# Mixing stage of a two-block transformer kernel: the chunked recurrence recast as one state map per chunk and eight-chunk sweeps

## The chip, the core and the metric

The kernel runs on one core of one Trainium2 chip. The metric is the device time of one execution in microseconds: 1955.51 us is the median of three runs of the kernel before (1954.65 to 1956.76). The profiled execution took 1951.49 us.

## What is computed

The input is 512 tokens of width 1024 in fp32. Two transformer blocks follow each other. Only one part of the second block is touched, the RWKV-7 recurrence: eight heads of 64, whose state is a 64 by 64 matrix that is updated at each of the 512 tokens.

```python
def step(state, inp):
    r_t, w_t, k_t, v_t, a_t, b_t = inp
    sa = jnp.einsum('bhvk,bhk->bhv', state, a_t)
    state = (state * w_t[:, :, None, :] + sa[..., None] * b_t[:, :, None, :]
             + v_t[..., None] * k_t[:, :, None, :])
    return state, jnp.einsum('bhvk,bhk->bhv', state, r_t)
```

Beside the recurrence, the same stage computes the input projections of the block, a second attention (stick-breaking, eight heads) and the output projection.

## The kernel before, in words

The kernel works with features on partitions and tokens on the free axis. Large products are "dense" matmuls: weights are split into a high and a low part (ScalarE makes `whi`, line 243, VectorE makes `wlo`, line 249), and each 128 by 128 block of weights meets 512 tokens in three passes that add up in a bank of PSUM called `mm`. PSUM has eight banks: two for `mm`, and in this stage three called `c` and three called `pt`.

**The recurrence in chunks.** The eight heads are taken two at a time, f = 0 to 3: one head on partitions 0 to 63 and one on 64 to 127. The 512 tokens are eight chunks of 64. `rw_solve` (line 1825) prepares one f. After the norms and the decays it turns three tiles into token order (`tok`, line 1868), forms two 64 by 128 matrices per chunk and head (`mat`, line 1901; masked by VectorE at line 1908) and inverts a unit triangular 64 by 64 matrix per chunk and head by doubling: five levels (line 1947), each with a first product (line 1951), a masked copy out of PSUM into `z` by VectorE (line 1955), a second set of products (lines 1961 to 1966), and additions into the running inverse `tmt` by VectorE (lines 1968 to 1974). `rw_scan` (line 1977) then walks through the eight chunks one after another, with three steps that wait for each other in each chunk: the sum of two products goes through ScalarE into `xc` (line 1994), the product with the inverse goes through ScalarE into `uc` (line 2004), and from that come the new state `st` (VectorE, line 2016) and the chunk's output (VectorE, line 2023).

**Corners of the array.** All these products are 64 by 64 in fp32, so each uses one quarter of the 128 by 128 array: rows by the partitions it reads, columns by the partitions it writes. `pair` (line 401) issues two of them, one per head, each from its half to the same half. `four` (line 409) adds two for another chunk whose result goes to the opposite half (`other`, line 418), so that four different corners are used. In the trace each fp32 matmul of this kind stands as two instructions.

**The order of the work.** The instruction order of TensorE is written out by a planner, `weave` (line 425), when the program is built. Its streams are generators: a step issues small products and the copies behind them, then yields the time at which the next step may run, by estimates (`after`, line 468, with the constants of `COST`). While a stream waits, the planner puts dense matmuls in, at least `MINF` = 4 at a time, out of a fixed supply per period (line 1792). `WORK` (line 23) says how much small work it expects in each of five periods, and sets how the dense supply is spread over them. Period f runs the solve of f beside the scan of f - 1; period 4 runs the last scan beside the stick-breaking attention (lines 1813, 1814). TensorE executes strictly in that order, so a small product that isn't ready holds back everything after it.

Of the kernel before, what the change touches and what calls it, by code (L numbers as in the profile page):

```python
# [22 lines left out]
WORK = (28e3, 40e3, 41e3, 40e3, 85e3)  # L23
# [78 lines left out]
def consts2():  # L102
# [16 lines left out]
    for b in (2, 4, 8, 16, 32):  # L119
        lv.append(((q // b % 2 == 1) & (g // b == q // b - 1)))  # L120
# [173 lines left out]
class K:  # L294
# [114 lines left out]
    def four(self, *g):  # L409

        t = self.clock
        for o, l, r in g:
            for hh in (0, 1):
                p = slice(64 * hh, 64 * hh + 64)
                self.mm(o(p), l(p), r(p), start=True, stop=True)
        self.clock = t + 55 + (self.clock - t) / 4

    def other(self, p):
        return slice(64 - p.start, 128 - p.start)

    def turn(self, o, x):

        self.pair(o, x, lambda p: self.ident[p, p], True, True)
# [1401 lines left out]
    def rw_solve(self, f, u, ag):  # L1825
# [42 lines left out]
        def tok(n, src):  # L1868
            ps = self.bank("c")
            for c in range(8):  # L1870
                cs = slice(64 * c, 64 * c + 64)
                self.turn(lambda p: ps[p, cs], lambda p: src[p, cs])
            d = t2(f"tok{n}")
            S.activation(d, ps, AF.Copy)
            self.after("S", 512)
            return d

        yield lambda: (f, 0) in u
# [6 lines left out]
        vt = tok(2, v)  # L1885
# [8 lines left out]
        kt = tok(1, kb)  # L1894
# [6 lines left out]
        def mat(n, src):  # L1901
            for half in (0, 1):
                ps = self.bank("c")
                for c4 in range(4):
                    c = 4 * half + c4
                    self.pair(lambda p: ps[p, 128 * c4:128 * c4 + 128], lambda p: src[p, 64 * c:64 * c + 64],
                              lambda p: ar[p, c].rearrange("p i t -> p (i t)"), True, True)
                V.tensor_tensor(mats[n][:, 4 * half:4 * half + 4], ps.rearrange("p (c n) -> p c n", c=4),
                                C["mar"].unsqueeze(1).to_broadcast([128, 4, 128]), op=OP.mult)
                x = self.after("V", 512)  # L1910
                yield self.clock if half == 0 else x
# [11 lines left out]
        bc = lambda x: x.unsqueeze(1).to_broadcast([128, 4, 64])  # L1923
        sw = self.other
        tt = [self.rp.tile([128, 2, 4, 64], F32, name=f"tmt{q}", tag=f"tmt{q}", bufs=2) for q in (0, 1)]
        zz = lambda q: t2(f"z{q}", 256, 1).rearrange("p (c t) -> p c t", t=64)
        e = zz(1)
        for q, d in ((0, tt[0][:, 1]), (1, e)):
            V.tensor_tensor(d, ab[:, 4 * q:4 * q + 4, 0:64], bc(C["m1t"]), op=OP.mult)
            V.tensor_tensor(d, d, bc(C["eye"]), op=OP.add)  # L1930
            x = self.after("V", 512)
        self.rws = dict(ar=ar, ab=ab, ak=ak, bt=bt, kt=kt, vt=vt, tt=tt, dec=dec, bon=bon)
        eight = lambda: self.bank("c").rearrange("p (i c t) -> p i c t", i=2, t=64)
        da, db = tt
        yield x
        pa, pb = eight(), eight()
        for c in range(4):
            self.turn(lambda p: pa[p, 0, c], lambda p: da[p, 1, c])
        for c in range(4):
            self.four((lambda p: pa[p, 1, c], lambda p: e[p, c], lambda p: self.ident[p, p]),  # L1940
                      (lambda p: pb[sw(p), 0, c], lambda p: self.ident[p, p], lambda p: e[p, c]))
        S.activation(da[:, 0], pa[:, 0], AF.Copy)
        S.activation(db[:, 0], pa[:, 1], AF.Copy)
        w = self.after("S", 512)
        S.activation(db[:, 1], pb[:, 0], AF.Copy)
        self.after("S", 256)
        for l in range(5):
            yield w
            pa, pb = eight(), eight()
            for c in range(4):  # L1950
                self.four((lambda p: pa[p, 0, c], lambda p: ab[p, c, 0:64], lambda p: da[p, 0, c]),
                          (lambda p: pb[sw(p), 0, c], lambda p: ab[p, 4 + c, 0:64], lambda p: db[p, 0, c]))
            za, zb = zz(0), zz(1)
            for z, ps in ((za, pa), (zb, pb)):
                V.tensor_tensor(z, ps[:, 0], bc(C["lev"][:, 64 * l:64 * l + 64]), op=OP.mult)
                w = self.after("V", 256)
            yield w
            pa, pb, pc = eight(), eight() if l < 4 else None, eight()
            if l < 4:
                for c in range(4):  # L1960
                    self.four((lambda p: pa[p, 0, c], lambda p: da[p, 1, c], lambda p: za[p, c]),
                              (lambda p: pb[sw(p), 0, c], lambda p: db[p, 1, c], lambda p: zb[p, c]))
            for c in range(4):
                self.pair(lambda p: pa[p, 1, c], lambda p: za[p, c], lambda p: da[p, 1, c], True, True)
            for c in range(4):
                self.pair(lambda p: pc[p, 0, c], lambda p: zb[p, c], lambda p: db[p, 1, c], True, True)
            if l < 4:
                V.tensor_tensor(da, pa, da, op=OP.add)
                V.tensor_tensor(db[:, 0], pb[:, 0], db[:, 0], op=OP.add)
                self.after("V", 512)  # L1970
            else:
                V.tensor_tensor(da[:, 1], pa[:, 1], da[:, 1], op=OP.add)
            w = self.after("V", 256)
            V.tensor_tensor(db[:, 1], pc[:, 0], db[:, 1], op=OP.add)
            self.after("V", 256)

    def rw_scan(self, f, u, o, g2, sg, w):

        nc, V, S, P, C = self.nc, self.nc.vector, self.nc.scalar, self.nc.gpsimd, self.C2
        ar, ab, ak, bt, kt, vt, tt, dec, bon = (w[k] for k in ("ar", "ab", "ak", "bt", "kt", "vt", "tt", "dec", "bon"))  # L1980
        t2 = self.rt
        st = std = None
        y = o
        for c in range(8):
            cs = slice(64 * c, 64 * c + 64)
            tc = tt[c // 4][:, 1, c % 4]
            at = self.other if c > 3 else lambda p: p
            b = self.bank("pt")[:, 0:64]
            self.pair(lambda p: b[at(p)], lambda p: ak[p, c, 0:64], lambda p: vt[p, cs], True, st is None)
            if st is not None:  # L1990
                yield w
                self.pair(lambda p: b[at(p)], lambda p: ar[p, c, 0], lambda p: st[p], False, True)
            x = t2("xc", 64)
            S.activation(x, b, AF.Copy)
            w = self.after("S", 64)
            if st is not None and c < 7:
                std = t2("std", 64)
                V.tensor_scalar(std, st, dec[:, c:c + 1], None, op0=OP.mult)
                self.after("V", 64)
# [90 lines left out]
```

## Time and profile before

| what | value |
|---|---|
| median of three runs | 1955.51 us |
| profiled execution, its own time | 1951.49 us |
| its span, first to last instruction | 1949.7 us |
| TensorE busy | 1864.8 us, 96% |
| VectorE busy | 1094.1 us, 56% |
| ScalarE busy | 797.5 us, 41% |
| GpSimd busy | 149.9 us, 8% |
| granted TensorE clock, mean | 0.979 |

The profile is of one execution. Busy times are of each engine alone. A matmul's row lasts from its start to its modelled end; the matmuls of one stream overlap, so what one costs is read from start to start. The mixing stage with the recurrence lies at 1165 to 1573 us of the span.

### The profile page before, as it was taken

Reading aid. Unit: us, or ns where it says so; the run is one execution under the profiler, and the core shown is the slowest. Engines: PE = TensorE matmul, PEld = TensorE weight load, DVE = VectorE, ACT = ScalarE, POOL = GpSimd, SP = SyncE. Lnnn points to the kernel's source line nnn. Section 1 sums busy time; section 2 is a strip of 40 time slices with the busy share of each in tenths; the row PEclk is TensorE's granted clock in tenths of the full one; section 3 lists DMA queues with packets and bytes.
Section 4 is the critical chain, followed back from the end, with each engine's and each line's share of the span. In section 5 each row is a group of like instructions: output and inputs, shape, how many; then the busy total and the mean of one; then the engine's idle time right before and its main releaser. Section 6 shows DMA issues by size and latency. Waiting matters only on the chain.

```text
span 1949.7 us, 27795 instructions
## 1 busy us (share of the span) xinstructions
PE 1864.8 (96%) x11552; PEld 1456.1 (75%) x11556; DVE 1094.1 (56%) x1843; ACT 797.5 (41%) x1385; POOL 149.9 (8%) x117
## 2 busy tenths in 40 slices
PE   5989999979999998999999999999999999999999
PEld 2766666758888886788888877776766778888887
DVE  7588875583434345543444556676667774444343
ACT  3666767343323233322322354343445753223231
POOL 4341110050000002000000000000001300000000
PEclk8999999889999998999999999999999999999999
DMA  7124214312223221222232231110100022222222
GB/s 300 57 87 140 78 65 152 113 61 92 103 90 105 89 106 65 87 93 101 88 107 87 89 124 55 45 45 24 40 18 33 22 87 96 99 92 103 92 98 92
DMA packets 27486, 171.56 MB, mean 88 GB/s; under 512 B 3168, under 2 KB 3680, under 8 KB 9184
## 3 DMA queue, kind: packets, MB, share of 16 engines
q1 hardware_dynamic: 23472, 163.44, 24.2%
q10 hardware_dynamic: 3888, 6.34, 1.0%
q8 instruction: 91, 1.49, 0.3%
q14 instruction: 35, 0.29, 0.0%
HBM read 167.67 MB, written 2.10 MB: 87 GB/s over the span
## 4 chain that ended last, share of the span: by engine, by line
PE 77%; DVE 3%; ACT 2%; POOL 1%; issue 1%; DMA 1%; ACTq 0%; POOLq 0%
PE ps_mm L339 43%; PE ps_s L339 23%; PE ps_c L339 5%; PE ps_pt L339 4%; PE ps_o L339 1%; ACT whi L243 1%; DVE wlo L249 1%; POOL xr L1332 0%; PE ps_pt L902 0%; POOL x L1381 0%; DMA mask<-in_mask 0%; DMA x<-in_x 0%; PE ps_mm L758 0%; DVE hl L1396 0%; DVE rs_v L510 0%
## 5 line engine op out<-in xcount | busy, mean ns | idle before, releaser
L243 ACT ACTIVATE whi<-w 128x1024 fp32r<-128x1024 f32 (+4 forms) x277 | 274.7, 994 | 740.7 <-PE ps_mm L339 440.8
L339 PE MATMUL ps_mm<-hh,whi 128*128 128x512 f32 x1304 | 519.9, 400 | 20.9 <-ACT whi L243 9.5
L339 PE MATMUL ps_mm<-hh,wlo 128*128 128x512 f32 x1304 | 518.1, 398 | 6.2 <-DVE wlo L249 6.2
L339 PE MATMUL ps_mm<-hl,whi 128*128 128x512 f32 x1304 | 519.2, 398 | 3.4 <-DVE hl L1339 2.0
L249 DVE TENSOR_TENSOR wlo<-w,whi 128x1024 fp32r<-128x1024 f32 (+7 forms) x316 | 322.3, 1025 | 149.3 <-ACT whi L243 148.8
L339 PEld LDWEIGHTS ps_mm<-hh,whi 128*128 128x128 f32 x1304 | 247.6, 190 | 82.3 <-ACT whi L243 12.8
L339 PEld LDWEIGHTS ps_mm<-hh,wlo 128*128 128x128 f32 x1304 | 247.4, 190 | 65.0 <-DVE wlo L249 10.1
L339 PEld LDWEIGHTS ps_mm<-hl,whi 128*128 128x128 f32 x1304 | 247.4, 190 | 60.3 <-DVE hl L1339 3.5
L339 PE MATMUL ps_s<-vl,whi 128*128 128x512 f32 x352 | 137.2, 390 | 0.0
L339 PE MATMUL ps_s<-vh,wlo 128*128 128x512 f32 x352 | 137.0, 389 | 0.0
L339 PE MATMUL ps_s<-vh,whi 128*128 128x512 f32 x352 | 136.6, 389 | 0.0
L1449 DVE SCALAR_TENSOR_TENSOR x<-ps_s,x 128x512 f32<-128x512 f32 x48 | 33.2, 692 | 129.2 <-PE ps_s L339 129.2
L1437 DVE TENSOR_TENSOR su<-ps_mm,rr 128x512 f32<-128x512 f32 x42 | 29.0, 691 | 133.1 <-PE ps_mm L339 133.1
L339 PE MATMUL ps_s<-uh,whi 128*128 128x512 f32 x256 | 99.6, 389 | 0.0
L339 PE MATMUL ps_s<-ul,whi 128*128 128x512 f32 x256 | 99.6, 389 | 0.0
L339 PE MATMUL ps_s<-uh,wlo 128*128 128x512 f32 x256 | 99.6, 389 | 0.0
L1436 DVE TENSOR_TENSOR sg<-ps_mm,rr 128x512 f32<-128x512 f32 x42 | 29.1, 692 | 97.3 <-PE ps_mm L339 93.2
L339 PEld LDWEIGHTS ps_s<-vl,whi 128*128 128x128 f32 x352 | 66.1, 188 | 14.3 <-DVE vl L783 0.7
L339 PEld LDWEIGHTS ps_s<-vh,wlo 128*128 128x128 f32 x352 | 66.1, 188 | 13.7
L339 PEld LDWEIGHTS ps_s<-vh,whi 128*128 128x128 f32 x352 | 66.1, 188 | 13.7
L876 ACT ACTIVATE P<-ps_s,st 128x512 f32<-128x512 f32 (+2 forms) x96 | 50.1, 528 | 15.7 <-DVE st L874 13.8
L1373 DVE TENSOR_TENSOR y<-y,ps_s 128x512 f32<-128x512 f32 x24 | 16.5, 688 | 70.0 <-PE ps_s L339 70.0
(576 smaller groups left out, 2762.5 us busy)
## 6 DMA issues: line engine op xcount, KB each, us to landing
w<-in_gu SPq DMA_DIRECT2D x44, 1024.0 KB, 4.8
w<-in_win SPq DMA_DIRECT2D x17, 1024.0 KB, 4.9
w<-in_wada SPq DMA_DIRECT2D x16, 1024.0 KB, 5.5
w<-in_wup SPq DMA_DIRECT2D x16, 1024.0 KB, 4.8
w<-in_wdn SPq DMA_DIRECT2D x16, 1024.0 KB, 4.8
w<-in_dn SPq DMA_DIRECT2D x16, 1024.0 KB, 4.8
wa<-in_wada SPq DMA_DIRECT2D x8, 1024.0 KB, 13.5
w<-in_dn SPq DMA_DIRECT2D x8, 768.0 KB, 4.2
```

The costliest lines, as they stand in the source:

```text
L243: self.nc.scalar.activation(hi[:, :n], src, AF.Copy)
L249: self.nc.vector.tensor_tensor(lo[:, o:m], src[:, o:m], hi[:, o:m], op=OP.subtract)
L339: self.last_pe = self.nc.tensor.matmul(o, l, r, start=start, stop=stop, skip_group_check=True)
L876: nc.scalar.activation(p[:, po:po + n], b[:, o:o + n], AF.Exp, bias=st[:, i:i + 1], accum_out=st[:, 4 + i:5 + i])
L1373: V.tensor_tensor(y[m], y[m], ps, op=OP.add)
L1436: V.tensor_tensor(g, pg, r, op=OP.mult)
L1437: V.tensor_tensor(v, pu, r, op=OP.mult)
L1449: V.scalar_tensor_tensor(self.x[m], ps, 0.5, self.x[m], op0=OP.mult, op1=OP.add)
```

## The change

The planner's `weave`, the dense work, the norms and the stick-breaking attention stay. The masks of the five levels (`lev`) are transposed. `WORK` is smaller.

A new helper, `sweep`, issues one product for all eight chunks and both heads (16 matmuls, or 32 with two terms). Each chunk of an operand or result has a "home": a rule such as `OWN` = (0, 0, 1, 1) says for chunk c, by c % 4, whether its two heads stand on their own halves of the partitions or on the exchanged ones. From the rule of the operands and that of the result, half of the chunks go straight and half turn, alternating, so that the four corners take their turns. The straight results go to one PSUM bank and the turned ones to another, 256 columns each, and each bank is read by an instruction of its own (`take`: ScalarE or VectorE).

In the solve, `tok` and `mat` and all levels become sweeps. The level mask is applied ahead, by GpSimd, to the left operand (`al`); VectorE adds the identity to `z`. Each level's last products hold the whole new inverse, so it is copied out and not added to. The two sets of products of a level share the two banks: columns 0 to 255 first, which are read, then columns 256 to 511. After the levels the solve adds two sweeps: the inverse times (`ak` times `v`) and the inverse times the turned `a`.

In the scan, the chunk's dependence on the state becomes one 64 by 64 map per chunk (`ab` times `b`, plus the identity), made for all chunks in one sweep, beside the part that does not depend on the state. What is left in series is one pair of products and one VectorE instruction per chunk, for six chunks. The rest follows in sweeps over all chunks.

```diff
-WORK = (28e3, 40e3, 41e3, 40e3, 85e3)
+WORK = (18e3, 25e3, 25e3, 25e3, 80e3)
...
+    OWN, KEY = (0, 0, 1, 1), (0, 0, 0, 0)
+
+    def inv(self, l):
+        return l % 2, 1 - l % 2, 0, 1
+
+    def sides(self, rows, out):
+        return [g for g in range(4) if rows[g] == out[g]], [g for g in range(4) if rows[g] != out[g]]
+
+    def sweep(self, banks, off, n, rows, out, *terms):
+        t, sides = self.clock, self.sides(rows, out)
+        for h in (0, 1):
+            for i in (0, 1):
+                for k, (l, r) in enumerate(terms):
+                    for bank, gs in zip(banks, sides):
+                        g, s = gs[i], off + n * (2 * h + i)
+                        for hh in (0, 1):
+                            a = self.quad(hh ^ rows[g])
+                            self.mm(bank[self.quad(hh ^ out[g]), s:s + n], l(a, 4 * h + g), r(a, 4 * h + g),
+                                    start=k == 0, stop=k == len(terms) - 1)
+        self.clock = t + 55 + (self.clock - t) / 4
+        return sides
...
+        def take(eng, dst, ps, gs):
+            if eng == "S":
+                S.activation(self.of(dst, gs), self.of(ps, None), AF.Copy)
+            else:
+                V.tensor_copy(self.of(dst, gs), self.of(ps, None))
+            return self.after(eng, 256)
...
-        yield from mat(1, kb)
+        w = mat(1, kb)
         yield x
-        bt = tok(0, bb)
-        yield from mat(0, bb)
-        ab, ak = mats
...
+        bt = tok(t3("tok0"), ch(bb), own)
+        yield w
+        w = mat(0, bb)
+        at = tok(t3("ee", 1), ar[:, :, 0], self.inv(5))
+        ab, ak = (m[:, :, 0:64] for m in mats)
+        ps = two()
+        for x, gs in zip(ps, self.sweep(ps, 0, 64, own, self.inv(5), (by(ak), by(vt)))):
+            take("S", ak, x[:, 0:256], gs)
...
+        lev = lambda l: P.tensor_tensor(al, ab, eight(C["lev"][:, 64 * l:64 * l + 64]), op=OP.mult)
...
         for l in range(5):
             yield w
...
+            ps = two()
+            now, new = self.inv(l), self.inv(l + 1)
+            sides = self.sweep(ps, 0, 64, own, now, (by(al), by(d0)))
+            for x, gs in zip(ps, sides):
+                V.tensor_tensor(self.of(z, gs), self.of(x[:, 0:256], None), self.wide(C["eye"]), op=OP.add)
                 w = self.after("V", 256)
+            if l < 4:
+                lev(l + 1)
+                x = self.after("P", 512)
             yield w
+            ps = two()
             if l < 4:
+                sides = self.sweep(ps, 0, 64, now, own, (by(d1), by(z)))
+                w = max(take(e, d0, y[:, 0:256], gs) for e, y, gs in zip("SV", ps, sides))
+                w = max(w, x)
+            sides = self.sweep(ps, 256, 64, now, new, (by(z), by(d1)))
+            for e, y, gs in zip("SV" if l == 4 else "SS", ps, sides):
+                x = take(e, d1, y[:, 256:512], gs)
+        yield x
+        ps = two()
+        for off, r, d, es in ((0, ak, d0, "SV"), (256, at, ab, "VS")):
+            sides = self.sweep(ps, off, 64, self.inv(5), own, (by(d1), by(r)))
+            for e, y, gs in zip(es, ps, sides):
+                x = take(e, d, y[:, off:off + 256], gs)
...
+        sides = self.sweep(ps, 0, 64, own, key, (by(ab), by(bt)))
+        self.sweep(ps, 256, 64, own, key, (by(kt), by(vt)), (by(bt), by(u0)))
...
+        for c in range(1, 7):
+            yield w
+            b = self.bank("pt")[:, 0:64]
+            self.pair(lambda p: b[p], lambda p: g[p, c], lambda p: st[p, c], True, True)
+            V.scalar_tensor_tensor(st[:, c + 1], b, dec[:, c:c + 1], h[:, c], op0=OP.mult, op1=OP.add)
+            w = self.after("V", 64)
+        yield w
...
+        for x, gs in zip(ps, self.sweep(ps, 0, 64, key, inv, (by(ar[:, :, 0]), by(st)))):
...
+        for e, x, gs in zip("SV", ps, self.sweep(ps, 0, 64, inv, own, (by(tc), by(ak)))):
...
+        yield w
+        pa, pb = two()
+        for h2 in (0, 1):
+            for i in (0, 1):
...
+                for b, b0, l, r, c, turned, start, stop in (
+                        (pa, s, vt, ak1, c, 0, True, False), (pb, s, vt, ak1, c2, 1, True, False),
+                        (pa, s, u0, ab1, c, 0, False, False), (pb, s, u0, ab1, c2, 1, False, True),
+                        (pa, s, st, ar[:, :, 1], c, 0, False, True), (pa, 256 + s, st, ar[:, :, 1], c2, 0, True, True)):
```

## Rows read from the trace of the kernel before

**Rows 1.** The page's first part: busy us, share of the span and instructions.

```profile
PE 1864.8 (96%) x11552; PEld 1456.1 (75%) x11556; DVE 1094.1 (56%) x1843; ACT 797.5 (41%) x1385; POOL 149.9 (8%) x117
```

**Rows 2.** Windows of the mixing stage: length, busy us (instructions) of PE, PEld, DVE, ACT, POOL.

```profile
1405.00:1440.00 35.00, 30.31 (x627) 22.98 (x627) 27.38 (x54) 15.64 (x25) 0.00 (x0) 1.00 0.08 25
...
sum 408.00, PE 392.58 PEld 289.25 DVE 286.87 ACT 193.46 POOL 29.57; mean PE 43.62 PEld 32.14 DVE 31.87 ACT 21.50 POOL 3.29
```

**Rows 3.** Windows of 10 us; behind POOL stands the granted clock.

```profile
1320.00:1330.00 10.00, 9.23 (x136) 6.69 (x134) 6.09 (x16) 1.55 (x6) 0.00 (x0) 0.66 0.01 3
...
1430.00:1440.00 10.00, 6.60 (x187) 5.47 (x182) 8.08 (x18) 3.44 (x6) 0.00 (x0) 1.00 0.23 80
...
1500.00:1510.00 10.00, 10.00 (x46) 6.40 (x46) 7.77 (x16) 6.10 (x14) 4.57 (x5) 0.73 0.00 0
1510.00:1520.00 10.00, 10.00 (x55) 8.58 (x54) 6.87 (x14) 7.92 (x17) 4.47 (x4) 0.83 0.01 2
...
1530.00:1540.00 10.00, 10.00 (x49) 8.10 (x49) 7.75 (x14) 7.00 (x15) 5.18 (x5) 0.83 0.01 2
```

**Rows 4.** Timeline of PE in the solve of f = 0: start us, length, what, count.

```profile
1209.04 0.40 PE L339 MATMUL ps_mm<-hh,wlo 128*128 128x512 f32 x1
1209.28 0.39 PE L339 MATMUL ps_mm<-hh,whi 128*128 128x512 f32 x1
1209.59 0.69 PE L339 MATMUL ps_c<-tmt,am 64*64 64x64 f32 x32
1210.22 0.50 PE L339 MATMUL ps_mm<-hl,whi 128*128 128x512 f32 x1
1210.56 0.40 PE L339 MATMUL ps_mm<-hh,wlo 128*128 128x512 f32 x1
...
1212.11 1.10 PE L339 MATMUL ps_c<-tmt,z 64*64 64x64 f32 x32
```

**Rows 5.** Tile ps_c: durations min/median/max in ns of single instructions.

```profile
L339 PE MATMUL ps_c<-tmt,am x640: 218/218/268, 1209.6 to 1435.7; 64*64 64x64 f32 x160
...
L339 PE MATMUL ps_c<-ar,ei x128: 269/269/320, 1196.6 to 1405.8; 64*64 64x128 f32 x128
```

**Rows 6.** Timeline of PE in `mat`.

```profile
1196.63 1.96 PE L339 MATMUL ps_c<-ar,ei 64*64 64x128 f32 x32
```

**Rows 7.** Who waited for whom at 1165 to 1573 us: total us, times, longest.

```profile
PEld ps_pt L339 <- ACT xc L1994: 3.5, 8, 0.7
PEld ps_pt L339 <- ACT uc L2004: 3.4, 7, 0.8
...
PE ps_pt L339 <- ACT uc L2004: 2.2, 6, 0.7
```

**Rows 8.** Timeline of all engines in the solve of f = 3, without dense work.

```profile
1432.72 0.47 PE L339 MATMUL ps_c<-hs_l,blk 128*128 128x512 f32 x1
...
1433.23 0.69 ACT L500 ACTIVATE rs_v<-ps_c,ec 128x512 f32<-128x512 f32 x1 [2.33 <-PE ps_c L339]
...
1434.45 0.69 DVE L1968 TENSOR_TENSOR tmt<-ps_c,tmt 128x512 f32<-128x512 f32 x1
...
1435.19 0.69 PE L339 MATMUL ps_c<-tmt,am 64*64 64x64 f32 x32 [0.33 <-DVE tmt L1968]
```

**Rows 9.** Groups of ACT by line at 1240 to 1440 us: busy, mean ns, idle before.

```profile
L505 ACT ACTIVATE rs_l<-rs_v 128x512 f32<-128x512 f32 x11 | 7.0, 632 | 3.0 <-DVE rs_v L503 2.8
...
L1942 ACT ACTIVATE tmt<-ps_c 128x256 f32<-128x256 f32 x3 | 1.2, 385 | 3.3 <-PE ps_c L339 3.3
```

**Rows 10.** Groups of DVE by line at 1240 to 1440 us.

```profile
L1908 DVE TENSOR_TENSOR am<-ps_c,mb 128x512 f32<-128x512 f32 x12 | 8.3, 690 | 15.2 <-PE ps_c L339 15.2
...
L521 DVE TENSOR_TENSOR hs_l<-hsq,hs_h 128x512 fp32r<-128x512 f32 x5 | 3.4, 685 | 0.0
```

**Rows 11.** Groups of DVE by line at 1487 to 1550 us.

```profile
L521 DVE TENSOR_TENSOR hs_l<-hsq,hs_h 128x512 fp32r<-128x512 f32 x3 | 4.2, 1406 | 0.0
```

**Rows 12.** Groups of POOL by line, whole span.

```profile
L1564 POOL TENSOR_TENSOR am<-am,am 128x512 fp32r<-128x512 f32 x4 | 6.7, 1687 | 2.2 <-DVE am L1559 2.2
```

More of the change, by code (lines that the diff above doesn't have):

```diff
@@ L119, in consts2 @@
     for b in (2, 4, 8, 16, 32):
[L120 removed]
+        lv.append(((g // b % 2 == 1) & (q // b == g // b - 1)))
     m["lev"] = np.concatenate(lv, 1)
@@ L1866, in rw_solve, with tok @@
         self.roots -= 1
[L1868 to L1875, printed above, removed]
+        own, key, quad = self.OWN, self.KEY, self.quad
+        unit = lambda p, c: self.ident[p, p]
+        by = lambda x: lambda p, c: x[p, c]
+        two = lambda: (self.bank("c"), self.bank("c"))
+        def take(eng, dst, ps, gs):
[4 more added lines that the diff above has]
+            return self.after(eng, 256)
+        def tok(d, src, to):
+            ps = two()
+            sides = self.sweep(ps, 0, 64, key, to, (by(src), unit))
+            for x, gs in zip(ps, sides):
+                take("S", d, x[:, 0:256], gs)
             return d
+        t3 = lambda n, bufs=2: ch(t2(n, 512, bufs))
         yield lambda: (f, 0) in u
@@ L1884, in rw_solve @@
         v = u[f, 2]
-        vt = tok(2, v)
+        vt = tok(t3("tok2"), ch(v), own)
         ar = self.rp.tile([128, 8, 2, 64], F32, name="ar", tag="ar", bufs=2)
@@ L1901, in mat @@
         def mat(n, src):
[L1902 to L1911, printed above, removed]
+            ps = two()
+            sides = self.sweep(ps, 0, 128, key, own, (by(ch(src)), lambda p, c: ar[p, c].rearrange("p i t -> p (i t)")))
+            for x, gs in zip(ps, sides):
+                V.tensor_tensor(self.of(mats[n], gs), self.of(x, None), self.wide(C["mar"]), op=OP.mult)
+                w = self.after("V", 512)
+            return w
         yield x
@@ L1932, in rw_solve @@
[L1932 to L1941, printed above, removed]
@@ new lines, in rw_solve @@
+        yield w
+        ps = two()
+        t = self.clock
+        same, turned = self.sides(own, self.inv(0))
+        S.activation(self.of(d1, same), self.of(z, same), AF.Copy)
+        for c in range(8):
+            for hh in (0, 1):
+                p = quad(hh)
+                self.mm(ps[0][p, 64 * c:64 * c + 64], z[p, c], self.ident[p, p], start=True, stop=True)
+            if c % 4 in turned:
+                s = 64 * (2 * (c // 4) + turned.index(c % 4))
+                for hh in (0, 1):
+                    p = quad(hh)
+                    self.mm(ps[1][quad(1 - hh), s:s + 64], self.ident[p, p], z[p, c], start=True, stop=True)
@@ L1944, in rw_solve @@
+        self.clock = t + 55 + (self.clock - t) / 3
+        S.activation(d0, ps[0].rearrange("p (c t) -> p c t", t=64), AF.Copy)
+        self.after("S", 256)
         w = self.after("S", 512)
-        S.activation(db[:, 1], pb[:, 0], AF.Copy)
-        self.after("S", 256)
+        take("V", d1, ps[1][:, 0:256], turned)
+        w = max(w, x)
         for l in range(5):
             yield w
[L1949 to L1955, printed above, removed]
+            ps = two()
+            now, new = self.inv(l), self.inv(l + 1)
+            sides = self.sweep(ps, 0, 64, own, now, (by(al), by(d0)))
+            for x, gs in zip(ps, sides):
+                V.tensor_tensor(self.of(z, gs), self.of(x[:, 0:256], None), self.wide(C["eye"]), op=OP.add)
@@ L1963, in rw_solve @@
[L1963 to L1972, printed above, removed]
```

141 lines of the change are left out of this document (67 added, 74 removed).

## The prediction, made before the change was run

> **What bounds the kernel now.** The page's first part comes first: TensorE is busy 96% of the span, no other engine over 56% [rows 1]. That number hides much, because a small matmul's row counts its whole way through the array. So the second view is the windows of the mixing stage: 392.58 of 408 us with TensorE busy, VectorE 286.87, ScalarE 193.46, GpSimd almost nothing [rows 2]. TensorE runs in the planner's order, so the length of this stage is, to first order, the sum of what stands in its queue: dense matmuls, small products, changes between the two, and waits. The third view is its timeline, which gives each of these a price [rows 4, 6]. The fourth is the end of a period, where the dense supply is used up: only 6.60 of 10 us busy [rows 3]. There the reader sees the chain of the solve itself, TensorE waiting for VectorE. Everything outside 1165 to 1573 us stays, and no DMA is moved.
>
> **Part 1, the small products.** A group's last start is its start plus its length less one instruction's duration (0.218 us [rows 5]). Sixteen matmuls on four corners take 0.69 - 0.22 = 0.47 us, 0.029 each; sixteen in pairs take 1.10 - 0.22 = 0.88 us, 0.055 each [rows 4]. With 128 columns, 16 in pairs take 1.96 - 0.27 = 1.69 us [rows 5, 6], 0.106 each, on four corners by the same ratio 0.053. Counting in the code for one f: before, 160 on four corners, 256 in pairs, 32 wide ones: 160 x 0.029 + 256 x 0.055 + 32 x 0.106 = 22.2 us. After, 488 in sweeps (360 in the solve, 64 more than before; 128 in the scan), 12 in the six state steps, 32 wide: 488 x 0.029 + 12 x 0.055 + 32 x 0.053 = 16.7 us. Two groups are not even: the start of the inverse has 16 straight and 8 turned, the outputs 32 and 16. A corner's own matmul takes 4 x 0.029 us, so 0.7 us come on top. 22.2 - 17.4 = 4.8 us, times four f: **-19 us**. The matmul count rises; the gain is all in the corners.
>
> **Part 2, going in and out of small work.** Around one such group the dense stream loses 0.07 us going in (0.31 from start to start where 0.24 is usual), 0.13 coming out (the last start at 1210.06, the next dense one at 1210.22, less 0.03) and 0.10 in the second dense matmul (0.34): 0.30 us [rows 4]. The solve has 17 such steps before and after. The scan has 24 before and 10 after: the state map, six links, three sweeps. 14 x 4 = 56 fewer, 17 us if each stood alone between dense work. Many steps of the scan stand right beside a step of the solve, where nothing is saved. I take three of five: **-10 us**, with 0 and -17 as ends.
>
> **Part 3, old waits that go.** TensorE's waits for the copies `xc` and `uc` are 3.5 + 3.4 + 2.2 = 9.1 us [rows 7]. Both copies go: **-9 us**. What is late next are the six state links, each a pair and one VectorE instruction, with at least four dense matmuls (0.24 each) put in between, as long as there is supply.
>
> **Part 4, new waits on one bank.** In each of the first four levels, and once after the levels, a sweep writes columns 0 to 255 of two banks, ScalarE or VectorE reads them, and the next sweep writes columns 256 to 511 of the same banks, with no dense work between. Nothing in the trace of before has this shape, so the price is bounded. If a bank may be written while its other half is read, it is 0. If not, TensorE stands from the last start until the copy has ended. The nearest rows: 0.22 for the last matmul to end, 0.04 until ScalarE starts (1433.19 to 1433.23), 0.385 for 256 columns [rows 9], 0.05 until TensorE goes on (VectorE's end at 1435.14, the matmul at 1435.19) [rows 8]. That is 0.70 us, less the usual 0.03: 0.67. Behind three activations of a norm of 0.63 us each [rows 9] it is 2.6. Twenty places: 0, 13 or 51 us. I take 0.67, since in the rows each matmul that needs a bank or a copy starts behind the reader's end: **+13 us**. The dense matmuls queued behind wait as well, and so do the copies of the new inverse. The Trainium skill, "PSUM — Partial Sum Buffer", section "PSUM bank collisions raise a hardware error", says that two engines must not touch the same bank and quarter of the partitions at one time, whichever columns. By that rule the 0 is out and the sum keeps its 13; no run here shows it.
>
> **Part 5, new waits for a free bank.** A sweep takes two of three `c` banks. In the solve the second `mat`, the new `tok` of a, and the product of `ak` and v follow each other without a yield. The second needs a bank that VectorE is still masking: 0.22 + 0.04 + 0.69 [rows 10] + 0.05 = 1.0 us; the third needs the one behind it, about the same. Two per f: **+8 us**. The ends are 0, if there is other work at that place, and 12, if the `tok` behind the first `mat` waits as well.
>
> **Part 6, costed at nothing.** ScalarE gets some 5 us more per f (about 30 copies of 0.385 us in place of 3 of 512 columns, 3 of 256 and 16 of 64). Its idle time in the stage, over 200 us [rows 2], covers that; without the cover each copy delays a level, which is the 2.6 us bound above. VectorE loses about as much. GpSimd does 20 masks of 512 columns; its nearest row takes 1.69 us [rows 12], and it has a level of several us for each, while it is idle from 1405 to 1440 us [rows 2]. What they may do to VectorE lies between 0 and 14 us, worked out among the rivals. The clock fell to half for a few stretches: the four windows lost 0.34 + 0.27 + 0.17 + 0.17 of 10 us, 9.5 us in all [rows 3]. Less dense-free time could give some of that back, denser small work could cost as much. I take 0 of -9.5 to +9.5. `WORK` only spreads the same dense supply.
>
> **The sum.** -19 - 10 - 9 + 13 + 8 = -17 us. The profiled execution took 1951.5 us (span 1949.7), so 1934.5; the median of the runs is 4.0 us above that execution, so on its scale 1938.5 us. A measurement of this kernel can tell about 0.2%, 4 us, from no change.
>
> **Rivals.** First, the new waits of parts 4 and 5 don't appear, because the copies are done sooner or a bank's halves don't hinder each other: -38 us, 1917.5. For it speaks that ScalarE is idle half the time; against it, that nothing is planned between the sweeps. Chance 0.17.
>
> Second, **slower**: the copies between the two sweeps of a level stand behind other work. Their place is ScalarE's queue, where a norm brings three activations of 0.63 us in a row [rows 9] and weights are converted too. The 28 new waits give away the gain as soon as they are 17 / 28 = 0.6 us longer on the mean than taken above; at 1.6 us longer, which is one norm chain mostly ahead of each, it is +28 us, 1966.5. Against it: a norm's root runs once at a time, a few times per f. Chance 0.12.
>
> Third, GpSimd's masks hold up VectorE. In the stretch where GpSimd works, an operation of VectorE with two operands in SBUF takes 1406 ns [rows 11] against 685 where it rests [rows 10]. If each of 20 masks costs the path 0.72 us, 14 us of the gain go: 1953, within 0.2%. Most reads of the levels come from PSUM, which speaks against it. The Trainium skill, "SBUF — State Buffer", section "Who interferes with whom", states this as a rule: a VectorE instruction with two SBUF inputs and a GpSimd one that reads SBUF exclude each other; rows 11 agree. Chance 0.10.
>
> Fourth, the period is as long as the solve's chain and not as TensorE's queue: shorter small work is only filled with waiting, as at 1430 to 1440 us [rows 3]: about 1955, no change. Against it stand 392.58 busy of 408 us [rows 2]. Chance 0.09. That the sweeps don't run on four corners is hardly one, since the rows already show that rate.
>
> **How the numbers follow.** The forecast has 0.52, with a range of its own from 1928 to 1950 (the ends of parts 2 and 5 and half of the clock's). Faster by over 0.2% are nearly all of it and the first rival, and a little of the third and fourth: 0.72. Within 0.2%: most of those two: 0.14. Slower: the second and the worse tail of the fourth: 0.14. The range goes from the first rival to beyond the third and fourth, 1916 to 1957; left out are the second and a clock that gains much.
>
> **What would show it.** In the profile after: 32 instructions of a sweep within 0.7 us in `mat`, `tok` and the second half of each level; no 64-column copies by ScalarE but the state's first; between the two product sweeps of a level a hole of about 0.7 us in TensorE's row, ended by ScalarE or VectorE; the outputs of f = 3 some 15 us earlier. Holes much over 1.2 us make it wrong upward, none at all downward, and a TensorE busy far less than now in the windows would speak for the fourth rival.

## The result, and the profile after

The changed kernel takes 1987.28 us (median of four runs, 1982.20 to 1991.63); the kernel before, run beside it, takes 1956.13 us (1954.65 to 1958.44). The ratio is 1.0157, interval 1.0129 to 1.0186: 31 us slower where 17 us faster was forecast. The profiled execution took 1982.2 us, its span is 1980.4 us and its mean granted clock 0.972 (before 1949.7 us and 0.979).

The page's first part, of after, answers to [rows 1]:

```profile
PE 1859.4 (94%) x12224; PEld 1453.3 (73%) x12228; DVE 1088.3 (55%) x1783; ACT 814.3 (41%) x1421; POOL 177.1 (9%) x141
```

TensorE has 672 more instructions and 5.4 us less busy time, in a span that is 30.7 us longer. Where they are, the windows say. Both kernels are cut at the same places: 1165 us, just behind the start of the stage (its first matmul, the product with `tw`, starts at 1162.7 us before and 1163.4 after), the last product of each of the four solves, and the end of the stage. Columns are the window, its length, busy us (instructions) of PE, PEld, DVE, ACT, POOL, then the granted clock, the DMA share and GB/s. First before, then after.

```profile
1165.00:1229.70 64.70, 61.29 (x822) 46.81 (x820) 42.92 (x79) 28.17 (x55) 0.00 (x0) 1.00 0.15 50
1229.70:1303.60 73.90, 73.75 (x1069) 54.22 (x1067) 52.32 (x109) 31.29 (x64) 0.00 (x0) 1.00 0.13 45
1303.60:1369.50 65.90, 62.89 (x1012) 46.09 (x1012) 42.38 (x94) 21.24 (x48) 0.00 (x0) 0.95 0.11 34
1369.50:1438.90 69.40, 64.06 (x1024) 46.61 (x1024) 51.93 (x108) 33.05 (x67) 0.00 (x0) 1.00 0.12 40
1438.90:1572.00 133.10, 129.58 (x812) 94.70 (x813) 96.57 (x192) 79.16 (x163) 29.57 (x24) 0.95 0.08 26
sum 407.00, PE 391.58 PEld 288.42 DVE 286.12 ACT 192.91 POOL 29.57; mean PE 78.32 PEld 57.68 DVE 57.22 ACT 38.58 POOL 5.91
```

```profile
1165.00:1237.50 72.50, 63.09 (x951) 47.58 (x950) 40.92 (x72) 33.39 (x75) 6.44 (x5) 0.95 0.13 45
1237.50:1323.80 86.30, 73.64 (x1236) 54.55 (x1236) 51.48 (x93) 36.59 (x73) 6.90 (x6) 0.94 0.11 38
1323.80:1394.20 70.40, 58.82 (x1183) 43.21 (x1181) 41.28 (x79) 26.03 (x57) 6.39 (x6) 0.98 0.10 32
1394.20:1467.50 73.30, 63.53 (x1188) 46.91 (x1188) 45.40 (x84) 32.98 (x69) 6.43 (x6) 0.91 0.09 27
1467.50:1602.00 134.50, 125.82 (x855) 92.31 (x854) 101.08 (x189) 81.39 (x158) 30.22 (x25) 0.95 0.09 30
sum 437.00, PE 384.91 PEld 284.57 DVE 280.17 ACT 210.37 POOL 56.38; mean PE 76.98 PEld 56.91 DVE 56.03 ACT 42.07 POOL 11.28
```

The stage grew from 407 to 437 us; behind it stand 377.7 and 378.4 us of span. The four periods with a solve grew from 273.9 to 302.5 us, the last part by 1.4. TensorE stood idle for 407 - 391.58 = 15.4 us before and for 437 - 384.91 = 52.1 us after. Its clock is worse as well: a window's lost clock, (1 - clock) x length, sums to 10 us before and 24 us after.

The change does what it says. Timeline of after in a setup and in one level (start us, length, what, count):

```profile
1203.01 1.10 PE L339 MATMUL ps_c<-ar,kk 64*64 64x128 f32 x32
...
1204.89 1.28 DVE L1938 TENSOR_TENSOR am<-ps_c,mb 128x512 f32<-128x512 f32 x2
1205.63 0.68 PE L339 MATMUL ps_c<-ident,ar 64*64 64x64 f32 x28 [1.41 <-DVE am L1938]
1206.34 1.57 POOL L1964 TENSOR_TENSOR al<-am,mb 128x512 f32<-128x512 f32 x1 [426.54 <-DVE am L1938]
...
1206.93 1.53 DVE L1961 TENSOR_TENSOR z<-z,mb 128x512 f32<-128x512 f32 x1
...
1223.65 0.69 PE L339 MATMUL ps_c<-tmt,al 64*64 64x64 f32 x32
1224.39 0.76 DVE L1994 TENSOR_TENSOR z<-ps_c,mb 128x256 f32<-128x256 f32 x2 [2.53 <-PE ps_c L339]
...
1224.96 0.92 PE L339 MATMUL ps_c<-z,tmt 64*64 64x64 f32 x32 [0.61 <-DVE z L1994]
1225.90 0.38 ACT L1897 ACTIVATE tmt<-ps_c 128x256 f32<-128x256 f32 x1 [2.62 <-PE ps_c L339]
...
1226.34 0.81 PE L339 MATMUL ps_c<-tmt,z 64*64 64x64 f32 x32 [0.46 <-ACT tmt L1897]
1227.08 0.50 PE L339 MATMUL ps_mm<-hl,whi 128*128 128x512 f32 x1
```

The 32 instructions of `mat` take 1.10 us where they took 1.96 [rows 6]; a sweep takes 0.69. Between the two sweeps of a level stands the hole of part 4: the last start is at 1224.96 + 0.92 - 0.22 = 1225.66, the next matmul at 1226.34, 0.68 us later, and ScalarE ends the wait. No dense matmul stands in the 2.7 us from 1223.65 to the hole's end.

Who TensorE waited for in the stage of after (total us, times, longest):

```profile
PE ps_c L339 <- ACT tmt L1897: 12.2, 24, 0.9
PE ps_c L339 <- DVE z L1994: 8.2, 12, 1.1
PE ps_c L339 <- DVE am L1938: 6.0, 6, 1.5
PE ps_c L339 <- DVE hs_l L542: 5.7, 2, 3.0
```

Of the 24 waits of the first row, 20 stand at the shared banks (10.5 us, read wait by wait in the timeline) and 4 ahead of the last level. The third row is the masked banks of part 5. The second and fourth have grown, and no step of the prediction names them: before, in the same view, the like of them were

```profile
PE ps_c L339 <- DVE z L1955: 3.2, 4, 1.9
PE ps_c L339 <- DVE hs_l L521: 2.9, 1, 2.9
...
PE ps_pt L339 <- ACT xc L1994: 1.2, 3, 0.5
```

### The profile page after: what moved, and what is told of

Same layout as the page of the kernel before. It is cut to its first block, busy times and chain, and to the rows that moved or that the text cites. A ratio compares the mean times of both kernels' runs of the same rounds, so it can differ in the third digit from the quotient of the medians.

```text
span 1980.4 us, 29186 instructions
## 1 busy us (share of the span) xinstructions
PE 1859.4 (94%) x12224; PEld 1453.3 (73%) x12228; DVE 1088.3 (55%) x1783; ACT 814.3 (41%) x1421; POOL 177.1 (9%) x141
## 5 line engine op out<-in xcount | busy, mean ns | idle before, releaser
L339 PE MATMUL ps_mm<-hh,whi 128*128 128x512 f32 x1304 | 520.8, 400 | 21.3 <-ACT whi L243 10.2
L1458 DVE TENSOR_TENSOR su<-ps_mm,rr 128x512 f32<-128x512 f32 x42 | 29.0, 691 | 133.1 <-PE ps_mm L339 133.1
L1964 POOL TENSOR_TENSOR al<-am,mb 128x512 f32<-128x512 f32 x20 | 25.7, 1285 | 620.2 <-DVE am L1938 545.0
L897 ACT ACTIVATE P<-ps_s,st 128x512 f32<-128x512 f32 (+2 forms) x96 | 50.0, 528 | 16.5 <-DVE st L895 14.6
```

The lines of the kernel that those rows point to most:

```text
L339: self.last_pe = self.nc.tensor.matmul(o, l, r, start=start, stop=stop, skip_group_check=True)
L897: nc.scalar.activation(p[:, po:po + n], b[:, o:o + n], AF.Exp, bias=st[:, i:i + 1], accum_out=st[:, 4 + i:5 + i])
L1458: V.tensor_tensor(v, pu, r, op=OP.mult)
L1964: lev = lambda l: P.tensor_tensor(al, ab, eight(C["lev"][:, 64 * l:64 * l + 64]), op=OP.mult)
```

## The experiments

Five theories stand against each other. A: the waits on shared banks carry the loss. B: the new `WORK` places the dense matmuls badly. C: the solve is the longer chain, and the planner's list puts the scan ahead of it. D: the solve's chain sets the length of a period, and dense work only covers it. Q, the premise of the prediction: the sum of TensorE's queue sets it. "Stage" below is the window from 1165 us to the place where the rest of the program begins.

**Both sweeps first (theory A).** In the levels and at the end, both sweeps that share banks are issued before either is read.

```diff
-                sides = self.sweep(ps, 0, 64, now, own, (by(d1), by(z)))
-                w = max(take(e, d0, y[:, 0:256], gs) for e, y, gs in zip("SV", ps, sides))
-                w = max(w, x)
+                first = self.sweep(ps, 0, 64, now, own, (by(d1), by(z)))
             sides = self.sweep(ps, 256, 64, now, new, (by(z), by(d1)))
+            if l < 4:
+                w = max(take(e, d0, y[:, 0:256], gs) for e, y, gs in zip("SV", ps, first))
+                w = max(w, x)
...
```

> In each level, and after the levels, both sweeps that share two banks are issued first and the copies of both halves follow; nothing else differs from the changed kernel. Theory A, the loss is the twenty holes in TensorE's queue where a sweep waits until the other half of its bank has been copied (about 0.73 us from start to start in the changed kernel): 20 x 0.7 = 14 us faster than the changed kernel, near 1973 us. Theory B, the loss is that the dense matmuls are spent early in each period and the levels run with nothing to cover VectorE and ScalarE: the copies of the running inverse then end at most 0.3 us earlier per level, 20 x 0.3 = 6 us, near 1981 us.

1964.21 us (ten runs, 1957.35 to 1969.52), ratio to before 1.0033 (1.0013 to 1.0053). The window of the stage, and the largest row of TensorE's waits:

```profile
1165.00:1583.00 418.00, 375.07 (x5408) 279.86 (x5407) 279.38 (x518) 209.96 (x434) 55.65 (x48) 0.96 0.11 36
```

```profile
PE ps_c L339 <- DVE tmt L1899: 10.7, 12, 1.6
```

23 us come back, more than the holes were worth: the profiled stage is 19 us shorter, of which 9.2 are idle time (52.1 to 42.9) and 9.8 busy time, with the clock at 0.96 for 0.95. Still 42.9 us are idle. The wait for ScalarE's copy between the sweeps is gone, and one for VectorE's copy, ahead of the next level or of the products behind the levels, stands in its place, 10.7 us. A is part of it, not all.

**The old `WORK` (theory B), in three kernels.** In the changed kernel and in the one with both sweeps first, `WORK` is put back; in the kernel before, the new one is put in.

```diff
-WORK = (18e3, 25e3, 25e3, 25e3, 80e3)
+WORK = (28e3, 40e3, 41e3, 40e3, 85e3)
```

> The changed kernel with the planner's WORK of before (28, 40, 41, 40, 85 in place of 18, 25, 25, 25, 80 thousand); the instructions are the same, only the places of the dense matmuls move. Theory B: dense matmuls are kept for the levels, the holes at the identity additions and at the norms shrink from some 25 us to some 10, 15 us faster than the changed kernel, near 1972 us. Theory A: within 4 us of the changed kernel, 1983 to 1991.

> Both edits of the two runs before. If A and B both hold and add up: near 1958 us, level with the kernel before. If they are the same waits seen twice: near 1970 us.

> The kernel before with the planner's WORK of the changed kernel (18, 25, 25, 25, 80 thousand). Theory B: spending the dense matmuls early costs this kernel too, 8 us or more, 1964 us or above. Theory A: within 4 us of before, 1952 to 1960.

Changed kernel: 1993.46 us (1991.12 to 1998.60), ratio 1.0189 (1.0158 to 1.0220), 6 us worse than with the new `WORK`, with intervals that overlap. Both sweeps first: 1974.53 us, ratio 1.0086 (1.0056 to 1.0116), 10 us worse. Kernel before with the new one: 1980.80 us (1977.36 to 1981.75), ratio 1.0118 (1.0089 to 1.0146). The stage of the first and of the last:

```profile
1165.00:1618.00 453.00, 396.89 (x5403) 296.01 (x5402) 276.22 (x517) 211.41 (x431) 55.34 (x48) 0.91 0.10 32
```

```profile
1165.00:1600.00 435.00, 400.50 (x4735) 300.46 (x4733) 284.27 (x578) 190.26 (x396) 29.00 (x24) 0.95 0.11 35
```

B falls in this form: the new numbers suit the new kernel better than the old ones. Whether others would suit it better still is not settled by that. But the last row says much of Q. Same instructions, same total of dense work, only in other places: 24 us. A queue in which the work sets the time could not do that. Idle time went from 15.4 to 34.5 us and the clock from 0.97 to 0.95.

**The solve ahead of the scan (C), a pause in the setup, `WORK` between.** All three stand on the kernel with both sweeps first.

```diff
-            self.weave(*scan, self.rw_solve(f, us, orw[f]), supply=...
+            self.weave(self.rw_solve(f, us, orw[f]), *scan, supply=...
```

> The kernel with both sweeps first, and in each period the planner asks the solve before the scan (their order in the list is exchanged). From the end of one inverse to the first token-order product of the next solve it took 35, 28 and 30 us there, against 24, 20 and 27 in the kernel before, with the norm's matmul standing behind scan steps and dense work that were ready first. Theory C, the solve is now the longer chain and is held up by the scan's place in the list: this stretch shrinks by 4 us or more in each of three periods, 10 to 15 us faster than with both sweeps first, near 1952 us. Theory A (waits on banks are all there was): within 4 us of it, 1960 to 1968.

```diff
         w = mat(0, bb)
+        yield w
         at = tok(t3("ee", 1), ar[:, :, 0], self.inv(5))
+        yield self.free["S"] + SEM2
```

> The kernel with both sweeps first, and a pause for the planner behind the second mask product and behind the token-order product of a, so that dense matmuls can stand where the next product waits for a free bank. Theory A: the holes there, 1.2 and 0.2 to 0.5 us, 6 us in all in that kernel's trace, go: 4 to 6 us faster, near 1959 us. If the dense matmuls are only taken from another place where they covered something (theory B): within 4 us, 1960 to 1968.

```diff
-WORK = (18e3, 25e3, 25e3, 25e3, 80e3)
+WORK = (23e3, 32e3, 33e3, 32e3, 82e3)
```

> The kernel with both sweeps first and WORK between the two sets (23, 32, 33, 32, 82 thousand). Same instructions, other places for the dense matmuls. Theory B, the place of the dense matmuls decides the rest of the loss and neither set fits: 8 us or more faster, 1956 us or below. Otherwise between the two runs at either set, 1964 and 1975 us.

The solve first: 1959.03 us (1956.14 to 1964.82), ratio 1.0029 (1.0013 to 1.0046), which can't be told from both sweeps first alone. The pause: 1962.25 us, ratio 1.0041 (1.0026 to 1.0056), no gain either. `WORK` between: 1969.03 us, ratio 1.0077 (1.0060 to 1.0094), some 5 us worse by the medians and 9 by the ratios. With the solve first the profile shows the move and where it went. The last product of the inverse, in the view of tile ps_c (min/median/max ns, first and last start us), with the solve first:

```profile
L339 PE MATMUL ps_c<-tmt,z x640: 218/218/312, 1211.0 to 1436.7; 64*64 64x64 f32 x160
```

and with both sweeps first alone:

```profile
L339 PE MATMUL ps_c<-tmt,z x640: 217/218/312, 1215.5 to 1450.8; 64*64 64x64 f32 x160
```

The last solve ends 14 us earlier, 11 us counted from the stage's first matmul (1161.4 us here, 1164.4 there). From its end to the stage's end, both sweeps first and then the solve first:

```profile
1453.40:1583.00 129.60, 124.22 (x852) 91.80 (x851) 100.62 (x190) 80.32 (x158) 29.70 (x25) 0.95 0.10 31
```

```profile
1439.20:1579.00 139.80, 131.44 (x853) 97.24 (x853) 99.35 (x191) 82.02 (x158) 28.46 (x25) 0.89 0.08 27
```

The same work takes 10.2 us more: 7.2 us more busy at a clock of 0.89 for 0.95, and 3.0 us more idle. So C is right about the solve and not about the time, which is given back behind it, in this execution for the most part with the clock.

**A third of the dense work left out (D against Q).** In the kernel before, and in the one with both sweeps first, one of the three passes is left out of the dense matmuls that the planner places. The edit reaches beyond the stage: other places of the program use the same helper.

```diff
-                self.mm(ps, w, x, start=k == 0 and j == 0, stop=k == n - 1 and j == 2)
+                if j != 1:
+                    self.mm(ps, w, x, start=k == 0 and j == 0, stop=k == n - 1 and j == 2)
```

> The kernel before, with the second of the three passes left out of the dense matmuls that the planner places in the mixing stage (the product of the weights' high part with the activations' low part; some 220 of 690 dense matmuls, 0.226 us each, 50 us of TensorE's time). The plan itself stays as it is, so each place has a third less dense work. Theory D, the length of the stage is set by the chain of the solve and dense work is cover: the fall is clearly less than 50 us, since waits come to light. Theory Q, TensorE's queue sets it: 45 us or more, 1910 us or below.

> The same omission in the kernel with both sweeps first (1964 us with all dense work). Theory D: it has less small work to stand beside the chain, so it falls by less than the kernel before does, by 10 us or more less. Theory Q: both fall by the same 45 to 50 us, near 1915 us.

Before with two thirds: 1951.73 us (ten runs, 1945.43 to 1956.38), ratio 0.9975 (0.9963 to 0.9987). Both sweeps first with two thirds: 1963.36 us (1959.23 to 1964.57), ratio 1.0030 (1.0014 to 1.0047). Ahead of the stage some 86 dense matmuls are gone too, and there the program got longer: the stage's first matmul starts at 1168.6 us for 1162.7, and at 1171.7 for 1164.4. So the stage is cut at that matmul here. The kernel before, whole and with two thirds:

```profile
1162.70:1572.00 409.30, 393.88 (x4741) 289.92 (x4740) 286.45 (x579) 194.16 (x399) 29.57 (x24) 0.97 0.11 37
```

```profile
1168.60:1567.00 398.40, 357.16 (x4515) 262.01 (x4514) 283.70 (x578) 192.67 (x398) 30.02 (x24) 0.93 0.11 38
```

Both sweeps first, whole and with two thirds:

```profile
1164.40:1583.00 418.60, 375.67 (x5410) 280.22 (x5409) 279.38 (x518) 209.96 (x434) 55.65 (x48) 0.96 0.11 36
```

```profile
1171.70:1581.00 409.30, 347.45 (x5188) 256.12 (x5186) 279.46 (x518) 210.26 (x434) 55.26 (x48) 0.88 0.11 38
```

and the last product of the inverse in the kernel before with two thirds:

```profile
L339 PE MATMUL ps_c<-tmt,z x640: 218/218/311, 1216.7 to 1434.4; 64*64 64x64 f32 x160
```

In the stage 226 and 222 dense matmuls are gone (4741 - 4515 and 5410 - 5188), at 0.23 us each from start to start [rows 4] some 51 us of TensorE's queue. The stage falls by 10.9 and by 9.3 us, the whole program by 4 and by 1 us (medians). The last solve starts its last product 266 us behind the stage's first matmul, where it did so 276 us behind it (1438.7 us). TensorE's busy time in the stage falls by 36.7 and 28.2 us instead of 51, at a clock of 0.93 for 0.97 and 0.88 for 0.96; its idle time rises by 25.8 us (15.4 to 41.2) and by 18.9 (42.9 to 61.9). Q falls: four fifths of the work that leaves the queue come back as waiting and as slower matmuls. D is nearer, for both kernels, but it is not the whole: a fifth of that work did come through, and the other thing that D foresaw, a fall smaller by 10 us or more in the second kernel, is not seen. How far the stage would have fallen at an unchanged clock, no run shows.

**Two more edits to the solve.** On top of the solve first: a pause behind the second `mat`, and the first level mask by VectorE and not by GpSimd.

```diff
         w = mat(0, bb)
+        yield w
...
-        lev(0)
-        x = self.after("P", 512, w)
+        V.tensor_tensor(al, ab, eight(C["lev"][:, 0:64]), op=OP.mult)
+        x = self.after("V", 512)
```

> The kernel with both sweeps first and the solve asked first, with two more edits: a pause behind the second mask product, and the first level's mask made by VectorE behind its two preparations of the inverse (in the changed kernel GpSimd makes it beside them, and the first of these takes 1533 ns on the mean where such an operation takes 685). If these two waits lie on the chain of the solve: 4 x (0.8 + 1.2) = 8 us faster than with the solve first, near 1951 us, a little faster than the kernel before. If the rest is a matter of cover (theory D, below): within 4 us of 1959.

1954.28 us (eleven runs, 1951.37 to 1960.07), ratio 0.9995 (0.9986 to 1.0004): level with the kernel before. The stage, and the part of it behind the last solve:

```profile
1165.00:1571.00 406.00, 367.05 (x5399) 275.01 (x5398) 279.69 (x519) 207.42 (x429) 47.90 (x44) 0.97 0.11 36
...
1443.50:1571.00 127.50, 123.36 (x850) 91.00 (x849) 101.63 (x190) 79.51 (x157) 28.89 (x25) 0.95 0.09 30
```

The second row holds a surprise. The two edits were to shorten the solves, but the last solve ends 4 us later than with the solve first alone; what came back, 12.3 us, is in the part behind, at a clock of 0.95 for 0.89. So this version is level, and the two links are not shown to be the reason.

The first row is the clearest of the study. Length and clock are those of before (407 us, 0.97). TensorE's busy time is 391.58 - 367.05 = 24.5 us less, which is about the work that parts 1 and 2 saved. Its idle time is 39.0 us for 15.4, 23.5 us more. The whole saving has turned into waiting.

**Less `WORK` still, and five dense matmuls at a time,** both on that kernel.

```diff
-WORK = (18e3, 25e3, 25e3, 25e3, 80e3)
+WORK = (17e3, 22e3, 22e3, 22e3, 80e3)
```

> The kernel with all fixes so far (both sweeps first, solve asked first, pause, first mask on VectorE; 1954 us) with WORK a little smaller (17, 22, 22, 22, 80 thousand). Of the sets tried the smaller one was the faster. If that goes on: 3 us or more faster, 1951 us or below, which would beat the kernel before. If the holes at the levels are the chain's own, they stay: within 4 us of 1954, and uncovered levels may add to it.

```diff
-SEM, SEM2, MINF = 250, 50, 4
+SEM, SEM2, MINF = 250, 50, 5
```

> The same kernel with five dense matmuls at the least in each wait instead of four. Theory D: each wait that has dense work left is covered by one more, but the supply is used up sooner and more levels run bare: within 4 us of 1954 or slower. If the short waits are under-covered: 3 us or more faster, 1951 us or below.

Less `WORK`: 1976.91 us (1968.37 to 1978.92), ratio 1.0095 (1.0079 to 1.0110), 20 us worse by the ratios. Five at a time: 1954.63 us (eleven runs, 1952.63 to 1955.53), ratio 0.9984 (0.9975 to 0.9993). By the ratios that is 3 us below before, the fastest version of the change that ran, and less than the 0.2% that counts here. The stage with less `WORK`:

```profile
1165.00:1593.00 428.00, 381.65 (x5405) 286.87 (x5404) 276.51 (x521) 209.63 (x434) 47.95 (x44) 0.92 0.10 34
```

Against the kernel without this edit, 22 us: 7.4 more idle (46.4 for 39.0) and 14.6 more busy, at a clock of 0.92 for 0.97. The instructions are the same. So the clock takes part in what a placement of the dense work costs. The forecasts of this run were 3 us faster, or within 4 us with some room for uncovered levels.

## Why the prediction was wrong

**The step that failed is the first one**, that "the length of this stage is, to first order, the sum of what stands in its queue", with work that is saved leaving the sum and waits that change only as parts 3 to 5 say. By its terms TensorE's work falls by 29 us and its waiting grows by 12 (-9 + 13 + 8). In the stage its busy time fell by 6.7 us (391.58 to 384.91) and its idle time grew by 36.7 (15.4 to 52.1). The premise was read from 392.58 busy of 408 us [rows 2]. But a planner that fills every wait with dense work makes TensorE busy whether or not it is the bound. With 51 us taken out of the queue, the stage of the kernel before gains 11.

The timeline shows which chain is the longer one: in each period that has a scan beside the solve, the solve ends last. Before, the scan's last product with the state ends at 1266, 1338 and 1404 us and the solve at 1304, 1370 and 1439; after, the scan at 1261, 1344 and 1418 and the solve at 1324, 1394 and 1468. So the solve, with the dense work and the scan's steps that stand ahead of its products, ends a period. That was the fourth rival, with 0.09, and the sign that was set for it came, a TensorE busy far less (384.91 of 437 us), though it foresaw no change in time; the row that spoke for it, 6.60 of 10 us at 1430 [rows 3], was the chain seen where the cover had run out.

**Parts 1 and 2**, -29 us, were right as work: a sweep of 32 instructions takes 0.69 us, `mat` 1.10 us, and the busy time at the same clock is 24.5 us less. They were wrong as time: in the version that is level with before (the two more edits to the solve) none of it came through.

**Part 3.** The waits for `xc` and `uc` went. But 6.9 of the 9.1 us [rows 7] are waits of the weight load (PEld), which overlaps the matmuls in the trace (288 us busy beside 392 in the 407); the matmuls' own waits for the two copies were 2.2 and 1.2 us. And since the scan does not end the period, waiting there need not be time of the result.

**Part 4** had the size of a hole right (0.67 us foreseen, 0.68 read), and nearly the total (13 us; the twenty waits are 10.5 us of idle time, or about 0.7 us each with the 0.22 us in which the last matmul ends, which the prediction counted in). The Trainium skill, "PSUM — Partial Sum Buffer", section "PSUM bank collisions raise a hardware error", led to the same side of the bounds, and the trace agrees: a copy's read ends each of the twenty waits, ScalarE's in all of them, with VectorE's behind it in two. Whether the chip or the program's own order asks for it, no run shows. But its worth was another matter: taking the holes out, with the clock that came along, gave 23 us.

**Part 5** was about right: six waits for the masked bank, 6.0 us, for 8.

**The second rival** has a wrong sum: 28 waits that are 1.6 us longer give 45 us, 28 above the kernel before, so 1983.5 us and not 1966.5. That would have been near the measured time by luck alone, since the waits of parts 4 and 5 were hardly longer than foreseen.

**Part 6** failed twice. That `WORK` "only spreads the same dense supply" is true and not harmless: 24 us in the kernel before, 20 in the last version. And the clock's lost time was taken as unchanged, with 9.5 us as the worse end; it went from 10 to 24 us. GpSimd was judged rightly: its masks take 1.29 us each (20 of them, 25.7 us from 1190 to 1470 us) and are hidden, but for the first of each f.

**The third rival** was real in one place of each solve. VectorE's groups in after, from 1190 to 1470 us (busy, mean ns, idle before):

```profile
L249 DVE TENSOR_TENSOR wlo<-w,whi 128x512 fp32r<-128x512 f32 x35 | 23.1, 685 | 1.7 <-ACT whi L243 1.6
...
L1961 DVE TENSOR_TENSOR z<-z,mb 128x512 f32<-128x512 f32 x4 | 6.1, 1533 | 0.1
```

The operation that adds the identity in the setup runs while GpSimd makes the first mask (1206.34 to 1207.91 in the timeline above) and takes 1533 ns, where `wlo`, also with two operands in SBUF, keeps 685: 4 x 0.85 = 3.4 us. The Trainium skill, "SBUF — State Buffer", section "Who interferes with whom", says as much, and the trace agrees for work at the same moment. The run with the two more edits to the solve confirms it: with the first mask made by VectorE behind it, the same operation takes 685 ns:

```profile
L1962 DVE TENSOR_TENSOR z<-z,mb 128x512 f32<-128x512 f32 x4 | 2.7, 685 | 0.0
```

**Why slower, and not just level.** The solve got new links: a wait inside each level, two sweeps at its end, a turned tile and a product more in its setup. It also starts later. From the end of one solve to the first `tok` of the next, the dense matmuls (tile ps_mm) are, before and after:

```profile
1229.70:1255.50 25.80, 14.52 (x50) 8.47 (x50) 1.38 (x2) 0.00 (x0) 1.00 0.13 42
1303.60:1324.50 20.90, 6.82 (x24) 4.04 (x24) 0.68 (x1) 0.00 (x0) 0.92 0.16 52
1369.50:1397.00 27.50, 15.52 (x56) 9.63 (x56) 2.08 (x3) 0.00 (x0) 1.00 0.11 40
```

```profile
1237.50:1272.30 34.80, 19.91 (x74) 13.27 (x74) 2.75 (x4) 0.00 (x0) 0.98 0.18 62
1323.80:1349.90 26.10, 7.19 (x25) 4.46 (x25) 1.38 (x2) 0.00 (x0) 0.93 0.13 42
1394.20:1423.50 29.30, 18.82 (x68) 12.06 (x68) 2.07 (x3) 0.00 (x0) 1.00 0.20 65
```

These stretches grew from 74.2 to 90.2 us and hold 37 more dense matmuls, 9 us more of busy time. From the first `tok` to the end of the solve the same three periods grew much less, from 135.0 to 139.8 us. The sums of the same view with both sweeps first (1234.1 to 1269.0, 1313.7 to 1340.7, 1382.9 to 1412.4 us) and with the solve first (1229.7 to 1257.7, 1306.3 to 1325.6, 1372.4 to 1393.7):

```profile
sum 91.40, PE 45.89 PEld 29.82 DVE 6.20 ACT 0.00; mean PE 15.30 PEld 9.94 DVE 2.07 ACT 0.00
```

```profile
sum 68.60, PE 39.84 PEld 25.93 DVE 5.49 ACT 0.00; mean PE 13.28 PEld 8.64 DVE 1.83 ACT 0.00
```

With both sweeps first the three solves themselves, up to the next of these windows and to 1452.9 us, take 127.4 us, less than before, and what that kernel still loses in these periods is the later start; with the solve first the stretches shrink and the solves grow to 140.4 us (the last ends at 1438.7). So in these three periods the later start is the larger part of the loss (16.0 us), and the longer solve the smaller (4.8 us); the first period, with no solve ahead of it, grew by 7.8 us. That the dense supply is used up ahead of the chain and then lacks beside it is the likely reason, argued from the 37 matmuls and not shown by a run. In numbers of the result: without the waits on shared banks 23 of the 31 us are back, and with the three further edits the other 7. In the profiles of these two versions the last solve ends at 1453.4 and 1443.5 us, and the part behind it takes 129.6 and 127.5 us, at a clock of 0.95 in both.

**What stays open.** Idle time and lost clock come together, and no run changed one alone, so how the 31 us divide between them isn't settled; nor is why the last part is granted 0.89 in one version and 0.95 in another with the same work. Nor is it known how much of the 31 us a better `WORK` would give back: four sets were tried on the change, and one step of it moved the last version by 20 us. That the scan's new form saves anything by itself was not tried. Nor was the solve's chain run with no dense work at all, which would give its bare length.

## What to carry to other kernels

Where a planner fills every wait of one engine with independent work, that engine's busy share does not tell the bound: take some of the filler away, in the stage in question alone, and see whether that stage follows, measured from its own first instruction. If it hardly does, look for the chain that ends last, and judge a change by when that chain starts and by what it adds to it; in this kernel, waits there outweighed the work saved elsewhere. The constants that place the filler belong to one kernel and have to be set anew for the next, since they moved the time here by as much as the change was meant to.

## What the runs showed of the hardware

Less work on TensorE went with a lower granted clock. With a third of the planned dense matmuls left out, the mean over the span fell from 0.979 to 0.963 in the kernel before, and from 0.975 to 0.951 in the one with both sweeps first; in the stage alone, from 0.97 to 0.93 and from 0.96 to 0.88. But idle time does not order the stretches by their clock. The fourth period of after, where TensorE is idle for 9.8 of 73.3 us, was granted 0.91, and the third, idle for 11.6 of 70.4 us, 0.98; the fourth of before, idle for 5.3 of 69.4 us, 1.00, and the last part of before, idle for 3.5 of 133.1 us, 0.95.

Four corners of the array at once halve the cost of small fp32 products, for 64 columns and, as had only been estimated, for 128: 32 instructions in 1.10 us for 1.96.
